# Output projection of one streaming-encoder layer: seven half products a row pair instead of eight, with token sums kept where the residual lay

## The chip, the cores and the metric

The kernel runs on one core of one Trainium2 chip. The metric is device time in microseconds for one call. Three runs of the kernel before took 1586.69, 1587.35 and 1587.35 us (median 1587.35). The profiled execution of the same kernel took 1586.78 us; from its first to its last instruction, its span, are 1585.1 us. Engines are named as in the profile: PE is the matrix engine (its weight loads are PEld), DVE the vector engine, ACT the scalar engine, POOL GpSimd, SP the queue that issues transfers.

## What is computed

One layer acts on 1056 tokens (1024 of a prompt, 32 of a sample) with 1024 channels. Only this part matters here:

```
merged = sigmoid(ga) * (ya @ w_br_att) + sigmoid(gm) * (ym @ w_br_mlstm)
x = x + gt1 * (merged @ w_out)            # the output projection
h2 = rmsnorm(x, g_ffn) * (1 + sc2) + sh2
g, up = split(h2 @ w_gate_up)             # the gated network follows
x = x + gt2 * ((silu(g) * up) @ w_down)
```

## The kernel before

Everything is kept transposed: 128 channels on the partitions, tokens along a row. The tokens are cut in three tiles of 352 (`TILES`, here t0, t1, t2; t2 holds 320 prompt and 32 sample tokens), the 1024 channels in eight blocks j of 128. A product in full precision is made from reduced ones: every weight and every operand is split into a high part (a rounding copy on ACT, L380) and a low part (what is left, a subtraction on DVE, L381). For each k block PE then does three passes: high weight by high operand, low weight by high operand, high weight by low operand (`PASSES`). A *unit* (L418) is one row block j times one token tile: 8 k blocks by 3 passes, 24 matmuls of 352 columns. A *half product* is four k blocks, 12 matmuls.

Weights come through a planner, `Weights`. A block has a load (SP, into one of 3 `wraw` buffers), a split (ACT and DVE, into `wsp` tiles of four k blocks, 4 of them) and a number of uses. When PE's program reaches a block (`W.use`), the planner emits the split of blocks up to `W.ahead` further on, as far as 4 `wsp` tiles hold them. `W.ahead` is 2 in the output projection and 4 after it. ACT, DVE and POOL each run their instructions strictly in the order in which the program emits them; only PE's order and theirs is written by hand, by emission.

Side work (`Side`) is a generator that is stepped while PE's matmuls are emitted: `side.start(gen, steps, ticks, delay)` spreads its steps over so many ticks, and there is a tick for every two k blocks, 6 matmuls. `side.drain` emits what is left at once.

The stages around the change, in order:

- *Merge* (L1626 on). For each j, a gate pair comes back from memory, and so does the residual `x2[j]`, all 1056 tokens (L1633). Two half units a tile, three DVE operations (L1639, L1641, L1642), then the result is split into `merged[j]` (L380, L381).
- *Output projection* (L1835 on). First all eight rows on t0, then all eight rows on t1 and t2: 24 units. After each unit DVE adds the product, times the gate `gt1`, onto the residual (L1842; this is called a *take* below; on t2 it is two pieces, 320 and 32 tokens), ACT squares the row (L1845, L1848), POOL adds the square to a sum (L1850), and SP stores the row to `xres` (L1861).
- *Second norm* (`second_norm`, L1672). For a tile: PE sums the squares over channels (`statistics`, L1662, and for the last row's square L1664), POOL takes the root, PE and ACT spread it over the partitions (L230, L233), and for each j DVE multiplies (L1694), ACT scales, shifts (L1697) and rounds (L1699), and DVE makes the low part (L1719) of `h2[j]`. For t0 it runs beside the projection's units on t1 and t2 (15 steps over 50 ticks); for t1 and t2 behind them, followed by `early_forms`, the operand sums of the gated network.

`xq` are four tiles that hold the residual of rows p and p+4 side by side. `h2` are eight `slots` buffers, taken when the second norm first needs them.

Of the kernel before, what the change touches and what calls it, by code (L numbers as in the profile page):

```python
# [17 lines left out]
P = 128  # L18
# [121 lines left out]
def hybrid_stream_step(  # L140
# [1428 lines left out]

    for w in w_merge + w_o[0] + w_o[1] + [w for ws in w_f for w in ws]:  # L1570
        W.add(w)
# [76 lines left out]
    sq_last = {}  # L1648
    h2 = []

# [21 lines left out]
    def second_norm(tiles):  # L1672
# [8 lines left out]
        for i, (lo, hi) in enumerate(tiles):  # L1681
# [41 lines left out]
    a_d = dr.tile([NF, P, T], F32, name="a_d")  # L1723
    thirds = [slice(lo, hi) for lo, hi in TILES]


# [107 lines left out]

    for pi, tiles in enumerate(parts):  # L1835
        if pi == 1:
            job = side.start(second_norm(parts[0]), 15, 50)
        for j in range(KD):
            for lo, hi in tiles:
                pt = unit(w_o[pi][j], 0, merged, lo, hi)  # L1840
                for c, a, b in col_segments(lo, hi):
                    dve.scalar_tensor_tensor(x2[j][:, a:b], pt[:, a - lo:b - lo], gt1[:, c, j:j + 1], x2[j][:, a:b],  # L1842
                                             op0=ALU.mult, op1=ALU.add)
                if j == 0:
                    act.activation(ss[:, lo:hi], x2[j][:, lo:hi], AF.Square)  # L1845
                else:
                    sq = third_tile()
                    act.activation(sq, x2[j][:, lo:hi], AF.Square)  # L1848
                    if j < KD - 1 or pi == 0:
                        pool.tensor_tensor(ss[:, lo:hi], ss[:, lo:hi], sq, op=ALU.add)  # L1850
                        if j == KD - 1:
                            sq_last[lo] = None
                    else:
                        sq_last[lo] = sq
                        if (lo, hi) == TILES[1]:


                            side.drain(job)
                            job = side.start(chain(second_norm(parts[1]), early_forms()), 9, 10)
            a, b = tiles[0][0], tiles[-1][1]  # L1860
            sp.dma_start(xres[j][:, a:b], x2[j][:, a:b])  # L1861

# [507 lines left out]
```

## Time and profile before

| what | value |
|---|---|
| median of three runs | 1587.35 us |
| the profiled execution | 1586.78 us |
| its span | 1585.1 us |
| PE busy | 1564.8 us, 10181 matmuls |
| DVE, ACT, POOL busy | 1107.0, 787.6, 420.5 us |
| granted PE clock over the span | 0.999 |
| output projection, first to last take | 797.7 to 889.1 us |

Busy times and shares are those of the profile's page; the line numbers there are those of the kernel before. A row of the timeline gives the start (us from the span's start), the length, the engine, the line, the operation, what it writes and reads, how many instructions are merged in it, and the engine's idle time before it with what ended that. Matmuls overlap: one of 352 columns lasts about 0.32 us, but the next starts half as much later.

### The profile page before, as it was taken

What the parts mean: (1) busy time and instruction counts of PE and PEld (TensorE: products, weight loads), DVE (VectorE), ACT (ScalarE), POOL (GpSimd) and SP (SyncE); (2) the same over time, 40 slices, a digit from 0 to 9 for tenths busy, and PEclk for the clock granted to TensorE, in tenths of its full rate; (3) what the DMA queues carried; (4) which work ended last, traced back from release to release, by engine and by line L of the source; (5) the groups of instructions that cost most, each with busy time, mean ns of one, the idle gap of its engine ahead of it and who ended that gap; (6) DMA issues with size and microseconds to landing.
All of it is one profiled execution on the core that took longest, in us unless ns stands there. A gap on an engine that the chain in (4) does not pass through costs nothing.

```text
span 1585.1 us, 27255 instructions
## 1 busy us (share of the span) xinstructions
PE 1564.8 (99%) x10181; PEld 1548.1 (98%) x10181; DVE 1107.0 (70%) x2270; ACT 787.6 (50%) x1730; POOL 420.5 (27%) x439
## 2 busy tenths in 40 slices
PE   8999999999999999999999999999999999999997
PEld 8999999999999999999999999999999999999997
DVE  3865655556767845446655699888898986799755
ACT  4765554544555545444434646544445444545443
POOL 0433343442223411000012100665665750000000
PEclk9999999999999999999999999999999999999999
DMA  9322233243122323575353312222232227427444
GB/s 376 131 76 78 88 104 98 93 132 106 42 91 74 88 78 102 120 275 173 112 157 113 94 55 67 82 77 98 68 93 83 69 89 248 137 80 253 129 137 156
DMA packets 176481, 187.08 MB, mean 118 GB/s; under 512 B 11766, under 2 KB 141466, under 8 KB 176222
## 3 DMA queue, kind: packets, MB, share of 16 engines
q1 hardware_dynamic: 173686, 183.50, 36.7%
q10 hardware_dynamic: 2664, 1.85, 0.4%
q8 instruction: 80, 1.31, 0.4%
q14 instruction: 51, 0.42, 0.1%
HBM read 151.15 MB, written 34.17 MB: 117 GB/s over the span
## 4 chain that ended last, share of the span: by engine, by line
PE 92%; DVE 4%; ACT 3%; issue 1%; POOL 0%; DMA 0%; ACTq 0%; DVEq 0%; POOLq 0%
PE mm L418 41%; PE psb L1903 18%; PE mm L1903 11%; PE psb L2285 3%; PE mm L971 3%; PE mm L2285 2%; PE psV L876 2%; PE psb L2149 2%; PE mm L329 2%; PE psS L817 1%; PE psT L844 1%; PE mm L2149 1%; DVE st L831 1%; PE psV L1205 1%; PE psT L1207 1%
## 5 line engine op out<-in xcount | busy, mean ns | idle before, releaser
L418 PE MATMUL mm<-s,wsp 128*128 128x352 f32 x4104 | 686.9, 324 | 0.3 <-DVE s L688 0.3
L418 PEld LDWEIGHTS mm<-s,wsp 128*128 128x128 f32 x4104 | 657.2, 188 | 2.1 <-DVE s L688 0.5
L381 DVE TENSOR_TENSOR wsp<-wraw,wsp 128x512 fp32r<-128x512 f32 (+1 forms) x280 | 236.1, 860 | 112.4 <-ACT wsp L380 110.4
L1903 PE MATMUL psb<-s,wsp 128*128 128x352 f32 x1611 | 271.4, 322 | 0.7 <-ACT wsp L380 0.7
L380 ACT ACTIVATE wsp<-wraw 128x512 fp32r<-128x512 f32 x336 | 199.7, 617 | 143.6 <-PE psb L1903 45.4
L1903 PEld LDWEIGHTS psb<-s,wsp 128*128 128x128 f32 x1611 | 260.6, 188 | 1.0 <-ACT wsp L380 1.0
L1903 PE MATMUL mm<-s,wsp 128*128 128x352 f32 x933 | 159.2, 322 | 0.7 <-DVE row L1941 0.7
L1903 PEld LDWEIGHTS mm<-s,wsp 128*128 128x128 f32 x933 | 151.2, 188 | 1.1 <-ACT wsp L380 1.0
L837 POOL TENSOR_SCALAR st<-st,mx 128x640 f32<-128x640 f32 (+5 forms) x72 | 53.3, 741 | 182.9 <-DVE mx L836 164.9
L1298 DVE CUSTOM_DVE_ANT_0 junk<-wa,t 128x512 bf16<-128x512 f32 x128 | 95.4, 746 | 2.8 <-DMA wa<-in_w_mod_dram 1.7
L381 POOL TENSOR_TENSOR wsp<-wraw,wsp 128x512 fp32r<-128x512 f32 x56 | 74.5, 1350 | 51.5 <-ACT wsp L380 49.2
L831 DVE CUSTOM_DVE_ANT_0 st<-psS,bias 128x640 f32<-128x640 f32 (+5 forms) x72 | 44.5, 618 | 57.9 <-PE psS L817 41.2
L832 ACT ACTIVATE st<-st,mx 128x640 f32<-128x640 f32 (+5 forms) x72 | 47.9, 666 | 63.7 <-DVE mx L831 63.6
L1850 POOL TENSOR_TENSOR t<-t,sl 128x352 f32<-128x352 f32 x19 | 18.0, 949 | 213.1 <-ACT sl L1848 213.1
L851 ACT ACTIVATE pT<-psT 128x640 fp32r<-128x640 f32 (+3 forms) x80 | 38.6, 493 | 64.2 <-PE psT L844 49.7
L2258 POOL TENSOR_TENSOR fst<-fst,mhalf 128x6 f32<-128x6 f32 x1 | 2.3, 2314 | 221.1 <-DVE fst L2257 221.1
L856 DVE TENSOR_TENSOR pT<-psT,pT 128x640 fp32r<-128x640 f32 (+3 forms) x80 | 44.0, 558 | 22.1 <-ACT pT L851 22.1
L1511 POOL TENSOR_TENSOR wraw<-wraw,raw 128x512 f32<-128x512 f32 x33 | 55.8, 1703 | 0.9
L971 PE MATMUL mm<-s,s 128*128 128x264 f32 (+3 forms) x432 | 54.5, 283 | 0.0
L2285 PE MATMUL psb<-s,wsp 128*128 128x352 f32 x330 | 54.2, 324 | 0.0
L2285 PEld LDWEIGHTS psb<-s,wsp 128*128 128x128 f32 x330 | 53.1, 188 | 0.1
L971 PEld LDWEIGHTS mm<-s,s 128*128 128x128 f32 (+1 forms) x432 | 51.9, 179 | 0.5
(381 smaller groups left out, 2457.5 us busy)
## 6 DMA issues: line engine op xcount, KB each, us to landing
wraw<-in_w_in_dram SPq DMA_DIRECT2D x37, 512.0 KB, 3.7
wraw<-in_w_gate_up_dram SPq DMA_DIRECT2D x33, 512.0 KB, 3.9
wa<-in_w_mod_dram SPq DMA_DIRECT2D x64, 256.0 KB, 2.7
wraw<-in_w_down_dram SPq DMA_DIRECT2D x32, 512.0 KB, 4.2
a_d<-t SPq DMA_DIRECT2D x22, 528.0 KB, 2.8
g_d<-t SPq DMA_DIRECT2D x16, 528.0 KB, 3.5
t<-g_d SPq DMA_DIRECT2D x16, 528.0 KB, 4.6
s<-in_w_ada_dram SPq DMA_DIRECT2D x16, 512.0 KB, 7.9
```

The source lines that it names most:

```text
L380: act.activation(dst[:, 0], src, AF.Copy)
L381: eng.tensor_tensor(dst[:, 1], src, f(dst[:, 0]), op=ALU.subtract)
L418: pe.matmul(pt[:, :hi - lo], wt[(w0 + k) // 4][:, a, (w0 + k) % 4], xt[k][:, b, lo:hi], start=(k == 0 and q == 0), stop=(k == n - 1 and q ...
L831: dve.tensor_tensor_reduce(so, sv, bi, -1.0, 3.0e38, ALU.add, ALU.min, mx[:n, 1:2])
L832: act.activation(st[:n, :w], st[:n, :w], AF.Exp, bias=mx[:n, 1:2], scale=-1.0, accum_out=mx[:n, 2:3])
L837: pool.tensor_scalar(st[:n, :w], st[:n, :w], mx[:n, 3:4], 1.0, op0=ALU.mult, op1=ALU.mult)
L971: pe.matmul(pt[:n, :wd], hs[k][:, a, i * P:i * P + n], whl[b][:, k, :wd], start=(k == 0 and q == 0), stop=(k == KD - 1 and q == 2))
L1298: dve.tensor_tensor_reduce(junk, wa, crow[:, c], 1.0, 0.0, ALU.mult, ALU.add, at)
L1511: self.eng.tensor_tensor(a(dst), a(x), a(y), op=op)
L1903: pe.matmul(acc, wt[:, a, k], x[k][:, b], start=(start and not onto and k == 0 and q == 0), stop=(stop and k == 3 and q == 2), skip_group_ ...
L2149: pe.matmul(acc, wt[k // 4][:, u, k % 4], piece_of[k, i][:, v], start=(k == 0 and q == 0), stop=(k == KP - 1 and q == 2))
L2285: pe.matmul(acc, wt[(k - k0) // 4][:, u, (k - k0) % 4], piece_of[k, 2][:, v], start=(k == 0 and q == 0), stop=(k == NF - 1 and q == 2))
```

## The change

Six of the eight rows, in the pairs (0, 4), (1, 5), (2, 6), are done two rows at a time. On t1 and t2 the pair's work is a two-by-two block product: two rows by two token tiles, over two halves of the channels, eight half products. The changed kernel does it with seven, by sums of weight blocks (`s1` to `s4`, made by `OutSeven.form`) and sums of token tiles (`T1` to `T4`, made by `sum_forms`), with results added onto each other in PSUM (`onto=True`). On t0 the pair still takes four half products. Rows 3 and 7 (`ALONE`) keep whole units.

The tokens' sums need merged values of t1 and t2 in full precision. The merge therefore writes them into `x2[j]`, where the residual used to be, and makes the sums in place during its last three rows (p = 0, 1, 2; p = 3 follows). They are then split into the `h2` buffers, which are taken right after the merge, by a side job `token_forms` of 19 steps over 22 ticks. Only t0 of the residual is loaded ahead; t1 and t2 are reloaded from memory when a piece's sums have been split (`form_low`, at T4). A take now happens for every half result that a row needs: nine for a pair where there were six. The planner's blocks for the pairs are half-blocks of one `wsp` tile, with one or two uses, and `W.ahead` is still 2 there. The second norm of t0 starts in the third pair, 15 steps over 14 ticks after a delay of 2.

```diff
+            def block(src, names=(), ld=lambda: None, uses=1):
+                def split(_):
+                    for n in names:
+                        form(n)
+                    t = wsplit_tile()
+                    split_to(t, src())
+                    return [t]
+                return [ld, split, uses, None, 1]
+
+            self.blocks = [
+                block(lambda: a(0, 0), ld=lambda: load(0), uses=2),
+                block(lambda: a(0, 1), ld=lambda: load(1), uses=2),
+                block(lambda: self.s["s2"], ("s1", "s2")),
+                block(lambda: a(1, 0)),
+                block(lambda: self.s["s3"], ("s3",)),
+                block(lambda: self.s["s1"], ("s4",)),
+                block(lambda: a(1, 1), uses=2),
+                block(lambda: self.s["s4"]),
+            ]
...
-        sp.dma_start(x2[j], x_t[j])
+        sp.dma_start(x2[j][:, :NT], x_t[j][:, :NT])
...
-            dve.tensor_tensor(ga[:, lo:hi], ga[:, lo:hi], gm[:, lo:hi], op=ALU.add)
-            split_to(mg[:, :, lo:hi], ga[:, lo:hi])
+            o = ga if lo == 0 else x2[j]
+            dve.tensor_tensor(o[:, lo:hi], ga[:, lo:hi], gm[:, lo:hi], op=ALU.add)
+            split_to(mg[:, :, lo:hi], o[:, lo:hi])
+            if j > 4:
+                sum_forms(j - 5, (("T1", "T3"), ("T2",), ("T4",))[TILES.index((lo, hi))])
...
+    def form_low(n, p, src, dst):
+        dve.tensor_tensor(dst[:, 1], src, f(dst[:, 0]), op=ALU.subtract)
+        if n == "T4":
+            for j in (p, p + 4):
+                sp.dma_start(x2[j][:, NT:], x_t[j][:, NT:])
...
+    def out_pair(j, u):
+
+        a00, a01, s2, a10, s3, s1, a11, s4 = seven_o[j].blocks
...
+        c = mmt()[:, :NT]
+        half(a00, ops["00"], c, stop=False)
+        half(a00, ops["B11"], u)
+        take(j, t2, u, False)
+        half(a01, ops["10"], c, start=False)
+        take(j, t0, c)
+        store(j, *t0)
+        take(j, t2, half(a01, ops["B21"], mmt()[:, :NT]))
...
+        half(s2, forms_o["T2"], u, onto=True)
+        take(j, t1, u, False)
+        c = mmt()[:, :NT]
+        half(a10, ops["00"], c, stop=False)
+        half(s3, forms_o["T3"], u, onto=True)
+        take(j + 4, t1, u, False)
...
+        v = half(s1, forms_o["T1"], mmt()[:, :NT])
+        take(j + 4, t1, v)
+        half(a11, ops["10"], c, start=False)
+        take(j + 4, t0, c)
+        store(j + 4, *t0)
+        if j == 2:
+            jobs.append(side.start(second_norm(parts[0]), 15, 14, 2))
+        half(a11, forms_o["T4"], u, onto=True)
+        take(j + 4, t2, u)
+        store(j + 4, NT, T)
+        half(s4, ops["B22"], v, onto=True)
+        take(j, t1, v)
+        store(j, NT, T)
+
+    job = side.start(token_forms(), 19, 22)
+    for w, j in zip(w_o[0], ALONE):
+        take(j, TILES[0], unit(w, 0, merged, *TILES[0]))
+        store(j, *TILES[0])
+    for j in range(3):
+        out_pair(j, (ps_s() if j % 2 == 0 else ps_t())[:, :NT])
+    for w, j in zip(w_o[1], ALONE):
+        for t in parts[1]:
+            take(j, t, unit(w, 0, merged, *t))
+            if j == ALONE[-1] and t == TILES[1]:
+                side.drain(jobs[0])
+                job = side.start(chain(second_norm(parts[1]), early_forms()), 9, 10)
+        store(j, NT, T)
```

How the order of instructions moves, at three places. First DVE, where the merge ends and the projection begins. Before (`L381 wsp` is the low part of a weight block, `L1842` a take, `L381 s` the low part of a merged row):

```order
L1642 TENSOR_TENSOR t_1171_8644<-t_1171_8644,t_1172_8645 128x352
L381 TENSOR_TENSOR s_1173_8649<-t_1171_8644,s_1173_8649 128x352
L381 TENSOR_TENSOR wsp_1185_8760<-wraw_1152_8432,wsp_1185_8760 128x512
L381 TENSOR_TENSOR wsp_1186_8761<-wraw_1152_8432,wsp_1186_8761 128x512
L1842 SCALAR_TENSOR_TENSOR x2_1083_7842<-mm_1188_8768,amod2_177,x2_1083_7842 128x352
L381 TENSOR_TENSOR wsp_1189_8796<-wraw_1164_8545,wsp_1189_8796 128x512
L381 TENSOR_TENSOR wsp_1190_8797<-wraw_1164_8545,wsp_1190_8797 128x512
L1842 SCALAR_TENSOR_TENSOR x2_1084_7843<-mm_1192_8804,amod2_177,x2_1084_7843 128x352
```

And now (`L1686` makes a token sum, `L1897` is the take, `L1945` the low part of a token sum, `wsp_1196` the first half-block of the first pair):

```order
L381 TENSOR_TENSOR s_1173_8657<-x2_1086_7845,s_1173_8657 128x352
L1686 TENSOR_TENSOR x2_1085_7844<-x2_1085_7844 128x352
L381 TENSOR_TENSOR wsp_1193_8780<-wraw_1152_8432,wsp_1193_8780 128x512
L381 TENSOR_TENSOR wsp_1194_8781<-wraw_1152_8432,wsp_1194_8781 128x512
L1686 TENSOR_TENSOR x2_1086_7845<-x2_1086_7845 128x352 x4
L1897 SCALAR_TENSOR_TENSOR x2_1086_7845<-mm_1195_8786,amod2_177,x2_1086_7845 128x352
L381 TENSOR_TENSOR wsp_1196_8819<-wraw_1164_8549,wsp_1196_8819 128x512
L1945 TENSOR_TENSOR s_1185_8771<-x2_1083_7842,s_1185_8771 128x352 x2
L1945 TENSOR_TENSOR s_1189_8775<-x2_1083_7842,s_1189_8775 128x352
L1897 SCALAR_TENSOR_TENSOR x2_1086_7845<-mm_1197_8822,amod2_177,x2_1086_7845 128x352
L381 TENSOR_TENSOR wsp_1201_8860<-wraw_1164_8549,wsp_1201_8860 128x512
```

Five token sums now stand ahead of the first take, and the low parts of the pair's weights stand one by one between takes and the low parts of token sums. Second, ACT where the second pair begins in the changed kernel (`L1906` squares a row after a take, `L380` is the high part of a weight half-block; `wsp_1218` and `wsp_1222` are a00 and a01, `wsp_1225` is s2, `wsp_1229` is a10):

```order
L1906 ACTIVATE sl_1216_9050<-x2_1083_7842 128x352
L1906 ACTIVATE sl_1217_9068<-x2_1083_7842 128x352
L380 ACTIVATE wsp_1218_9072<-wraw_1211_8992 128x512
L1906 ACTIVATE sl_1219_9088<-x2_1083_7842 128x352
L380 ACTIVATE wsp_1222_9094<-wraw_1211_8992 128x512
L380 ACTIVATE wsp_1225_9127<-t_1223_9123 128x512
L1906 ACTIVATE sl_1226_9143<-x2_1084_7843 128x352
L1906 ACTIVATE sl_1228_9162<-x2_1084_7843 128x352
L380 ACTIVATE wsp_1229_9165<-wraw_1214_9018 128x512
```

Before, a square and two high parts of a whole block alternate there, and the block is needed a unit later; now a half-block's high part stands behind the squares of takes that PE's previous half product but one releases. Third, DVE in the last unit pair, row 7, with the second norm of t0 (`L1754` its multiplication, `L1779` its low part) around the take of row 7 on t1 (`mm_1282`):

```order
L381 TENSOR_TENSOR wsp_1279_9602<-wraw_1262_9447,wsp_1279_9602 128x512
L381 TENSOR_TENSOR wsp_1280_9603<-wraw_1262_9447,wsp_1280_9603 128x512
L1754 TENSOR_TENSOR x2_1086_7845<-x2_1086_7845,t_1184_8770 128x352
L1779 TENSOR_TENSOR s_1187_8773<-x2_1085_7844,s_1187_8773 128x352
L1754 TENSOR_TENSOR x2_1083_7842<-x2_1083_7842,t_1184_8770 128x352
L1779 TENSOR_TENSOR s_1188_8774<-x2_1086_7845,s_1188_8774 128x352
L1754 TENSOR_TENSOR x2_1084_7843<-x2_1084_7843,t_1184_8770 128x352
L1779 TENSOR_TENSOR s_1189_8775<-x2_1083_7842,s_1189_8775 128x352
L1754 TENSOR_TENSOR x2_1085_7844<-x2_1085_7844,t_1184_8770 128x352
L1779 TENSOR_TENSOR s_1190_8776<-x2_1084_7843,s_1190_8776 128x352
L1897 SCALAR_TENSOR_TENSOR x2_1086_7845<-mm_1282_9610,amod2_177,x2_1086_7845 128x352
```

In the kernel before, that norm was spread over all of the second part, and about one of its operations stood between two takes; now eight of them stand in a row ahead of this one.

More of the change, by code (lines that the diff above doesn't have):

```diff
@@ L1568, in hybrid_stream_step @@
     w_d1 = [[weight([down(a, b, j)], b - a, 1) for a, b in chunks] for j in range(KD)]
-    for w in w_merge + w_o[0] + w_o[1] + [w for ws in w_f for w in ws]:
+    for w in w_merge + w_o[0] + [w for x in seven_o for w in x.blocks] + w_o[1] + [w for ws in w_f for w in ws]:
         W.add(w)
@@ L1628, in hybrid_stream_step, with sum_forms @@
     merged = []
+    thirds = [slice(lo, hi) for lo, hi in TILES]
+    def sum_forms(p, names):
+        x, y = x2[p], x2[p + 4]
+        one, two = thirds[2], thirds[1]
+        forms = {"T1": (x[:, one], x[:, two], x[:, one]), "T3": (x[:, two], y[:, two], x[:, two]),
+                 "T2": (y[:, two], y[:, two], x[:, one]), "T4": (y[:, one], y[:, one], y[:, two])}
+        for n in names:
+            o, u, v = forms[n]
+            dve.tensor_tensor(o, u, v, op=ALU.subtract)
     for j in range(KD):
@@ L1648, in hybrid_stream_step @@
     sq_last = {}
-    h2 = []
+    h2 = [slot([P, 2, T], F32R) for _ in range(KD)]
     def third_tile():
@@ L1723, in hybrid_stream_step @@
     a_d = dr.tile([NF, P, T], F32, name="a_d")
-    thirds = [slice(lo, hi) for lo, hi in TILES]
     FORMS = [[None] * 4 for _ in range(15)]
@@ L1833, in hybrid_stream_step @@
     normed = {}
[L1835 to L1861, printed above, removed]
@@ new lines, in take @@
+    def take(j, t, pt, last=True):
+        lo, hi = t
+        for c, a, b in col_segments(lo, hi):
+            dve.scalar_tensor_tensor(x2[j][:, a:b], pt[:, a - lo:b - lo], gt1[:, c, j:j + 1], x2[j][:, a:b],
+                                     op0=ALU.mult, op1=ALU.add)
+        if not last:
+            return
+        rows_done[lo] = rows_done.get(lo, 0) + 1
+        if rows_done[lo] == 1:
+            act.activation(ss[:, lo:hi], x2[j][:, lo:hi], AF.Square)
+        else:
+            sq = third_tile()
+            act.activation(sq, x2[j][:, lo:hi], AF.Square)
+            if rows_done[lo] < KD or lo == 0:
+                pool.tensor_tensor(ss[:, lo:hi], ss[:, lo:hi], sq, op=ALU.add)
+                sq = None
+            if rows_done[lo] == KD:
+                sq_last[lo] = sq
@@ new lines, in store, with token_forms @@
+    def store(j, a, b):
+        sp.dma_start(xres[j][:, a:b], x2[j][:, a:b])
+    rows_done, jobs = {}, []
+    forms_o = {}
+    def token_forms():
+        one, two = thirds[2], thirds[1]
+        where = {"T1": (0, one), "T3": (0, two), "T2": (4, two), "T4": (4, one)}
+        home = {"T2": (0, two), "T3": (0, one), "T1": (4, one), "T4": (4, two)}
+        sum_forms(3, ("T1", "T3"))
+        yield
+        sum_forms(3, ("T2", "T4"))
+        yield
+        order = [(n, 0) for n in ("T2", "T3", "T1", "T4")]
+        order += [(n, p) for n in ("T2", "T3", "T1", "T4") for p in range(1, 4)]
+        behind = []
+        for n, p in order:
+            dp, c = where[n]
+            hp, hc = home[n]
+            src, dst = x2[p + dp][:, c], h2[p + hp][:, :, hc]
+            forms_o.setdefault(n, [None] * 4)[p] = dst
+            act.activation(dst[:, 0], src, AF.Copy)
+            if behind:
+                behind.pop()()
+            behind.append(lambda n=n, p=p, src=src, dst=dst: form_low(n, p, src, dst))
+            yield
+        behind.pop()()
@@ new lines, in form_low, with half @@
+    def form_low(n, p, src, dst):
[3 more added lines that the diff above has]
+                sp.dma_start(x2[j][:, NT:], x_t[j][:, NT:])
+    def half(w, x, acc, start=True, stop=True, onto=False):
+        wt, = W.use(w)
+        for k in range(4):
+            for q, (a, b) in enumerate(PASSES):
+                pe.matmul(acc, wt[:, a, k], x[k][:, b], start=(start and not onto and k == 0 and q == 0),
+                          stop=(stop and k == 3 and q == 2), skip_group_check=onto)
+            if k % 2 == 1:
+                side.tick()
+        W.used(w)
+        return acc
```

34 lines of the change are left out of this document (31 added, 3 removed).

## The prediction

> **What bounds the kernel now.** I read the page first, then the busy times of the output projection by stretches, then its groups of instructions, then the timeline where the merge ends.
>
> ```profile
> PE 1564.8 (99%) x10181; PEld 1548.1 (98%) x10181; DVE 1107.0 (70%) x2270; ACT 787.6 (50%) x1730; POOL 420.5 (27%) x439
> ...
> PE 92%; DVE 4%; ACT 3%; issue 1%; POOL 0%; DMA 0%; ACTq 0%; DVEq 0%; POOLq 0%
> ```
>
> PE is the bound: 99% busy, 92% of the chain that ended last. In the projection, the stretches (columns: PE, PEld, DVE, ACT, POOL busy; granted clock; DMA share; GB/s) show no gap in PE and the others half idle:
>
> ```profile
> 797.00:830.00 33.00, 33.00 (x208) 33.00 (x207) 18.77 (x27) 12.82 (x25) 6.66 (x7) 1.00 0.60 178
> 830.00:860.00 30.00, 30.00 (x191) 29.98 (x190) 12.46 (x25) 10.27 (x20) 6.69 (x7) 1.00 0.34 112
> 860.00:890.00 30.00, 30.00 (x193) 30.00 (x192) 16.08 (x35) 13.71 (x27) 6.70 (x7) 1.00 0.34 107
> ```
>
> So each matmul removed is worth its pace, and each wait that PE gets is lost whole. The question is only whether the new order feeds PE in time.
>
> **What is removed.** The groups of 760 to 960 us give the pace:
>
> ```profile
> L418 PE MATMUL mm<-s,wsp 128*128 128x352 f32 x1075 | 174.5, 323 | 0.0
> ```
>
> 174.5 us / 1075 = 0.162 us a matmul. Three pairs save one half product of 12 each: 36 x 0.162 = **5.8 us**. A half product is 1.95 us, a unit 3.9.
>
> **What is added, and its price.** The timeline around the first take gives the links of the chain by which a weight block reaches PE:
>
> ```profile
> 795.63 0.53 DVE L381 TENSOR_TENSOR s<-t,s 128x352 fp32r<-128x352 f32 x1 [0.56 <-ACT s L380]
> 796.15 1.29 DVE L381 TENSOR_TENSOR wsp<-wraw,wsp 128x512 fp32r<-128x512 f32 x2
> ...
> 797.75 0.58 DVE L1842 SCALAR_TENSOR_TENSOR x<-mm,amod,x 128x352 f32<-128x352 f32 x1 [0.30 <-PE mm L418]
> 798.43 0.50 ACT L1845 ACTIVATE t<-x 128x352 f32<-128x352 f32 x1 [1.79 <-DVE x L1842]
> 798.83 1.14 ACT L380 ACTIVATE wsp<-wraw 128x512 fp32r<-128x512 f32 x2
> 799.48 1.29 DVE L381 TENSOR_TENSOR wsp<-wraw,wsp 128x512 fp32r<-128x512 f32 x2 [1.15 <-ACT wsp L380]
> ...
> 801.59 0.58 DVE L1842 SCALAR_TENSOR_TENSOR x<-mm,amod,x 128x352 f32<-128x352 f32 x1 [0.81 <-PE mm L418]
> 802.78 0.95 POOL L1850 TENSOR_TENSOR t<-t,sl 128x352 f32<-128x352 f32 x1 [158.24 <-ACT sl L1848]
> 803.26 1.62 DVE L381 TENSOR_TENSOR wsp<-wraw,wsp 128x512 fp32r<-128x512 f32 x2 [1.08 <-ACT wsp L380]
> ```
>
> From it: DVE to ACT 0.10; ACT's square holds it 0.40; a high part lasts 0.62 (two in 1.14, so 0.52 apart); ACT to DVE 0.03; a low part lasts 0.69 and holds DVE 0.60; a take 0.58, holding DVE 0.5. Beside POOL's addition the two low parts take 1.62 in place of 1.29. More holds, from later rows:
>
> ```profile
> 832.97 0.71 DVE L1842 SCALAR_TENSOR_TENSOR x<-mm,amod,x 128x320 f32<-128x320 f32 x2 [0.85 <-PE mm L418]
> 917.05 1.08 DVE L1739 TENSOR_TENSOR sl<-sl,x 128x352 f32<-128x352 f32 x2
> ...
> 918.48 0.52 DVE L1739 TENSOR_TENSOR sl<-x 128x352 f32<-128x352 f32 x1
> 918.91 0.52 DVE L1752 TENSOR_TENSOR s<-sl,s 128x352 fp32r<-128x352 f32 x1
> L1433 DVE TENSOR_TENSOR t<-wraw,wraw x8: 684/686/693, 1372.8 to 1466.0; 128x512 f32<-128x512 f32 x8
> ```
>
> A two-piece take 0.71; a 352-column sum or low part holds DVE 0.43, one that needs the one before it 0.56; a weight sum, by the down projection that sums weight blocks in the same way, lasts 0.69.
>
> The changed order has 32 more 352-column and 12 more 512-column two-input operations on DVE, 9 more takes (three of them in two pieces) and 16 more rounding copies on ACT: about 32 x 0.43 + 12 x 0.6 + 6 x 0.5 + 3 x 0.71 = 26 us of DVE in a stretch where it is busy 47 of 93 us. As a total that hides. It does not hide by order: a pair's block is a half-block, PE spends 1.95 us on one with a single use, the planner is at most one block ahead, and its split stands in line behind takes that wait for PE. Once PE waits for a high part, it also waits for the low part: its second pass needs it, so 0.03 + 0.69 - 0.16 = **0.56** more, or 0.95 when POOL adds beside it.
>
> *First pair*, on the clock of before. Unit boundaries on PE are near 797.55 and 801.39 (takes at 797.75 and 801.59, each 0.04 after the end of a pass of 0.32 whose successor starts 0.16 after it); a weight load is wanted 0.16 earlier, so a00 at 801.23. DVE now has one sum before the low parts that stood at 796.15 and four behind (0.43 + 3 x 0.56): first take at 799.85, square at 800.5, high part of a00 done 801.55: 0.3 late, plus 0.56. Then s2: three low parts (1.3), take, square, high and low part of a01 (805.8), four low parts (1.75), the two-piece take (0.7), two sums (1.4), high part done 810.3. PE has used a00 and a01 twice each and wants s2 at 801.55 + 0.56 + 4 x 1.92 = 809.8: 0.5 late, plus 0.56. Then a10: its high part stands on ACT behind the square of the next two-piece take, which DVE reaches after s2's low part, two low parts, a take and another: done 814.65 against 812.8, 1.9 late, plus 0.56. Then s3: 0.95, plus 0.56; s1: 0.2. Together **6.1** (4.5 to 7.5, by one step of 0.5 to 0.7 more or less in the queue).
>
> The reload stands in this too: the two-piece take, at 807.5, needs x2[0] back. Its transfer can go when T1's low part is done, near 803.6. Nearest rows:
>
> ```profile
> t<-g_d SPq DMA_DIRECT2D x13, 528.0 KB, 4.4
> ...
> x<-in_x_dram SPq DMA_DIRECT2D x3, 528.0 KB, 7.2
> ```
>
> The reload has 352 KB, two thirds of these: 3 to 5 us, landing 806.6 to 808.6. I take it as just in time; at the far end it adds 1.1, inside the 7.5.
>
> *Second and third pair.* No token sums are left, DVE has room, but two places in each run the same chain against one half product: a00 behind the square of the take of T4, and a10 behind that of B21. From the end of the pass: 0.04 + 0.71 (take) + 0.10 + 0.40 (square) + 0.62 + 0.03 = 1.90. The pass ends 0.32 after its start, the load is wanted 1.92 after it: 0.3 late, plus 0.56 or 0.95 (POOL adds the same square just then). s3's low part behind its sum: 0.57. Per pair 0.3 + 0.3 + 0.57 + 2 x (0.56 to 0.95) = 2.3 to 3.1; **5.6** for two. Row 3's whole block, behind the last pair in the same way: **0.8** (0.6 to 1.0).
>
> *Second norm of t0.* Its 15 steps now go into 14 ticks of 6 matmuls, 0.97 us a step, in place of 50. Rows on what a step needs:
>
> ```profile
> 853.15 0.50 ACT L1699 ACTIVATE s<-x 128x352 fp32r<-128x352 f32 x1
> 853.56 0.48 ACT L1848 ACTIVATE sl<-x 128x352 f32<-128x352 f32 x1
> 853.95 0.67 ACT L1697 ACTIVATE x<-x,amod 128x352 f32<-128x352 f32 x1
> 854.64 0.50 ACT L1699 ACTIVATE s<-x 128x352 fp32r<-128x352 f32 x1
> ```
>
> 0.69 and 0.41, 1.1 us of ACT a row, more than a step; and weight splits and squares stand between. What is late next is the statistics of t1: PE's L1664 matmul needs the square of row 7. From the broadcast's transposes to that matmul PE has 60 matmuls, 9.7 us. ACT has a square and the copy (1.1), the wait for DVE's first product (1.0), seven rows (7.7), a square and two high parts (1.4), the wait while DVE makes their low parts before the next product (1.8), the square itself (0.5): 13.5. PE waits **3.5** (2.0, if the two waits cover each other, to 4.2). Behind it in PE's queue stands the rest of row 7 on t2, then the gated network.
>
> At no cost: the merge loads a third of the residual, the stores are cut differently, eight residual loads of 528 KB become eight of 176 and eight of 352, at a DMA share of 0.60 or less. If that cover went, a w_out block would land late: the second of pair 1 is issued behind the last reloads, some 10 us before its first sum, against the 4 to 7 us of the rows above.
>
> *Sum:* -5.8 + 6.1 + 5.6 + 0.8 + 3.5 = +10.2. On the profiled execution (1586.8: 1585.1 of span and 1.7 around it) that is 1597.0, on the median of 1587.35 it is 1597.5. Forecast **1597**. With all low ends +5.9, with all high ends +13.1: 1593 to 1601 for this case.
>
> **A rule that speaks against the change.** The clock column reads 1.00 all through the projection, but here are the rows of PE's first work and of the end:
>
> ```profile
> 5.00:10.00 5.00, 4.87 (x23) 1.00 1.03 414
> 10.00:15.00 5.00, 5.00 (x44) 1.00 1.03 407
> 1580.00:1586.00 6.00, 0.00 (x0) 0.55 0.56 188
> ```
>
> After an idle start, PE makes 23 matmuls in its first 5 us and 44 in the next; at the end, idle again, the grant is 0.55. So an idle stretch of some microseconds seems to cost about (44 - 23) / 44 x 5 = 2.4 us of pace afterwards. The Trainium skill, in "TensorE: Matmul & The Clock Gate" (Why this matters for your kernels), says that a PE gap of more than about 3 us halves the clock again; by that the wait of the statistics, if over its bound, would cost those us more, and by these rows it may. No row shows a gap of 2 to 4 us in mid-kernel.
>
> **Rivals.** *The full gain* (other side): the split chain is not on PE's path, since DVE's and ACT's shares leave room and PE's gaps are absorbed: 1587.35 - 5.8 = 1581.6. Faster from the point where the waits sum under 5.8, a third of mine. For: no PE gap in 93 us before, where the same blocks alternate. Against: there a block was a unit ahead (the low parts of 799.48 serve a unit that starts at 801.39). *Half the waits*: the chains of 1.90 + 0.32 against 1.92 are so close that 0.3 less in each removes the first lateness, and s2's row keeps a margin; then 3.5 + 2.5 + 0.4 + 2 = 8.4, less 5.8: about 1590. *A colder PE or a late reload*: 10.2 plus 2.4 and up to 3 more for the reloads: 1600 to 1603. That fewer matmuls are not issued is excluded: the order has 8220 of 352 columns against 8256.
>
> **How the numbers follow.** Forecast 0.56, full gain 0.09, half the waits 0.15, colder or late 0.20. This kernel's measurement can tell 0.2%, 3.2 us, from no change: 1584.2 to 1590.5. The full gain gives faster 0.09; half the waits splits, 0.08 within; the rest is slower, 0.83. Range 1589 to 1603: it leaves out the full gain and the ends of the others.
>
> **What would show it.** PE's waits in the profile of the changed kernel: psS and mm of the half products waiting for ACT and DVE `wsp`, some 20 times, 0.2 to 2 us each, summing to 12, with half of it in the first pair; and one wait of psV for ACT's square of 2 to 4 us. Fewer than 6 us of PE waits between 793 and 900, or a take that waits for the reload, would make me wrong in size; the granted clock under 1.00 there would decide for the colder PE.

## The result: 1601.12 us, 0.9% slower

| | before | after |
|---|---|---|
| median, runs | 1587.35 us, 6 runs (1586.69 to 1587.52) | 1601.12 us, 6 runs (1600.40 to 1601.83) |
| the profiled execution | 1586.78 us | 1600.70 us |
| its span | 1585.1 us | 1599.0 us |

The ratio is 1.0088, with a 95% interval from 1.0075 to 1.0101. The forecast was 1597, slower, with a range from 1589 to 1603.

In the profile after, PE's waits in the output projection, in groups (engine, line, what it waited for: us in total, times, longest):

```profile
PE mm L1956 <- DVE wsp L381: 3.8, 6, 1.0
PE psV L1726 <- ACT sl L1906: 3.7, 1, 3.7
PE mm L1956 <- ACT wsp L380: 1.4, 1, 1.4
PE psS L1956 <- ACT wsp L380: 1.1, 2, 0.7
PE psS L1956 <- DVE wsp L381: 0.9, 3, 0.3
PE psT L1956 <- DVE wsp L381: 0.3, 1, 0.3
PE mm L418 <- DVE wsp L381: 0.3, 1, 0.3
```

Before, the same view of this stretch was empty. There are fourteen short waits for halves of weight blocks, where some twenty with a sum of 12 us were forecast, and the one long wait of the statistics. The short ones sum to 7.8 here, but their sizes are too small: ends of matmuls are modelled, so a pause counts only from the modelled end of the pass before, and some are not shown at all. The timeline of PE tells it by the starts:

```profile
796.83 4.80 PE L418 MATMUL mm<-s,wsp 128*128 128x352 f32 x29
801.65 0.43 PE L1956 MATMUL mm<-s,wsp 128*128 128x352 f32 x1
802.38 2.03 PE L1956 MATMUL mm<-s,wsp 128*128 128x352 f32 x11 [0.30 <-DVE wsp L381]
804.24 2.08 PE L1956 MATMUL psS<-s,wsp 128*128 128x352 f32 x12
...
814.91 0.43 PE L1956 MATMUL mm<-s,wsp 128*128 128x352 f32 x1 [1.42 <-ACT wsp L380]
815.64 2.04 PE L1956 MATMUL mm<-s,wsp 128*128 128x352 f32 x11 [0.30 <-DVE wsp L381]
...
826.89 2.44 PE L1956 MATMUL mm<-s,wsp 128*128 128x352 f32 x13
829.95 2.03 PE L1956 MATMUL mm<-s,wsp 128*128 128x352 f32 x11 [0.62 <-DVE wsp L381]
...
839.66 0.43 PE L1956 MATMUL mm<-s,wsp 128*128 128x352 f32 x1
841.05 2.03 PE L1956 MATMUL mm<-s,wsp 128*128 128x352 f32 x11 [0.96 <-DVE wsp L381]
...
875.85 2.11 PE L1956 MATMUL mm<-s,wsp 128*128 128x352 f32 x12
...
878.33 0.41 PE L418 MATMUL mm<-s,wsp 128*128 128x352 f32 x1
879.03 4.96 PE L418 MATMUL mm<-s,wsp 128*128 128x352 f32 x29 [0.29 <-DVE wsp L381]
...
893.82 0.28 PE L1724 MATMUL psV<-ones,t 128*128 128x1 f32 x2
897.75 0.58 PE L1726 MATMUL psV<-ones,sl 128*128 128x1 f32 x2 [3.65 <-ACT sl L1906]
...
909.61 0.28 PE L1724 MATMUL psV<-ones,t 128*128 128x1 f32 x2
...
973.68 1.60 PE L2056 MATMUL psb<-s,wsp 128*128 128x352 f32 x9
```

The row of 814.91 holds one pass; the next starts 0.73 later, where 0.16 is normal. So this pause for a low part is 0.57, of which 0.30 is shown. The same places before (the statistics of t1, those of t2, and the first product of the gated network's second part):

```profile
886.23 0.28 PE L1662 MATMUL psV<-ones,t 128*128 128x1 f32 x2
...
895.48 0.28 PE L1662 MATMUL psV<-ones,t 128*128 128x1 f32 x2
...
959.55 1.76 PE L1903 MATMUL psb<-s,wsp 128*128 128x352 f32 x10
```

The account follows from these starts, at 0.16 a matmul and 1.92 a half product.

- *First pair.* It is due at 796.83 + 29 x 0.16 = 801.47 and ends at 826.89 + 1.92 = 828.81. That is 27.34 for 11 half products (21.12): 6.2 of waits.
- *Second and third pair.* They end at 875.85 + 1.92 = 877.77, 48.96 later, for 42.24: 6.7.
- *Up to the statistics of t1.* These begin 7.6 later than before. The saved matmuls are 5.8, so all waits up to there are 13.4. Beside the 6.2 and 6.7 above, some 0.6 belong to row 3 (its first passes start at 878.33 and 879.03, 0.70 apart, and the one behind them 0.1 late) and 0.1 to a later start; that is 13.6, the same within the rounding of these steps.
- *From the statistics of t1 to those of t2.* 15.79 in place of 9.25, so 6.54 more. The gap is 3.65 of it. The other 2.9 go somewhere else, and the stretches behind the gap in the profile after say where (PE, PEld, DVE, ACT, POOL busy; clock; DMA share; GB/s):

```profile
897.70:903.70 6.00, 5.95 (x24) 5.95 (x25) 1.76 (x8) 2.13 (x5) 1.01 (x1) 0.50 0.05 21
903.70:910.00 6.30, 6.30 (x44) 6.28 (x42) 4.65 (x8) 5.60 (x10) 0.00 (x0) 1.00 0.66 185
```

The granted clock is 0.50 behind the gap: 24 matmuls in 6 us (ten of them the statistics' one-column ones), then 44 in 6.3. The trace's clock record has it at 0.5 for 6.83 us, from 896.86 on. PE idles in the first 0.9 of them; half of the other 5.9 is 3.0, against the 2.9 that are missing.

- *Behind that.* From the statistics of t2 to the gated network's second part both kernels take 64.07. The kernel after is 14.1 behind there and 13.9 at the end, so no more than 0.2 is won or lost anywhere else.

### The profile page after: what moved, and what is told of

Its sections match the earlier page's. It is cut to its first block, busy times and chain, and to the rows that moved or that the text cites. A ratio compares the mean times of both kernels' runs of the same rounds, so it can differ in the third digit from the quotient of the medians.

```text
span 1599.0 us, 27237 instructions
## 1 busy us (share of the span) xinstructions
PE 1567.1 (98%) x10145; PEld 1544.8 (97%) x10145; DVE 1131.2 (71%) x2326; ACT 794.9 (50%) x1746; POOL 420.4 (26%) x439
## 4 chain that ended last, share of the span: by engine, by line
PE 86%; DVE 6%; ACT 4%; DMA 2%; issue 1%; POOL 0%; SPq 0%; ACTq 0%; DVEq 0%; POOLq 0%
PE mm L418 35%; PE psb L2056 18%; PE mm L2056 11%; PE psb L2438 3%; PE mm L971 3%; PE mm L2438 2%; PE psV L876 2%; PE psb L2302 2%; PE psS L817 1%; DVE wsp L381 1%; PE psT L844 1%; DMA s<-in_w_ada_dram 1%; PE mm L2302 1%; PE mm L1956 1%; ACT wsp L380 1%
## 5 line engine op out<-in xcount | busy, mean ns | idle before, releaser
L418 PE MATMUL mm<-s,wsp 128*128 128x352 f32 x3672 | 619.6, 325 | 0.6 <-DVE wsp L381 0.3
L418 PEld LDWEIGHTS mm<-s,wsp 128*128 128x128 f32 x3672 | 589.7, 189 | 2.6 <-DVE s L688 0.5
L381 DVE TENSOR_TENSOR wsp<-wraw,wsp 128x512 fp32r<-128x512 f32 (+1 forms) x268 | 226.8, 861 | 114.5 <-ACT wsp L380 112.0
L380 ACT ACTIVATE wsp<-wraw 128x512 fp32r<-128x512 f32 x324 | 193.4, 617 | 144.3 <-PE psb L2056 44.1
L2056 PEld LDWEIGHTS psb<-s,wsp 128*128 128x128 f32 x1611 | 260.6, 188 | 1.0 <-ACT wsp L380 1.0
L2056 PE MATMUL mm<-s,wsp 128*128 128x352 f32 x933 | 159.2, 322 | 0.7 <-DVE row L2094 0.7
L2056 PEld LDWEIGHTS mm<-s,wsp 128*128 128x128 f32 x933 | 151.2, 188 | 1.1 <-ACT wsp L380 1.0
L381 POOL TENSOR_TENSOR wsp<-wraw,wsp 128x512 fp32r<-128x512 f32 x56 | 74.0, 1340 | 51.9 <-ACT wsp L380 49.6
L380 ACT ACTIVATE s<-x 128x352 fp32r<-128x352 f32 x84 | 37.4, 487 | 35.0 <-DVE x L1702 35.0
L380 ACT ACTIVATE wsp<-t 128x512 fp32r<-128x512 f32 x44 | 27.4, 630 | 52.7 <-DVE t L1570 19.8
```

The source lines that it names most:

```text
L380: act.activation(dst[:, 0], src, AF.Copy)
L381: eng.tensor_tensor(dst[:, 1], src, f(dst[:, 0]), op=ALU.subtract)
L418: pe.matmul(pt[:, :hi - lo], wt[(w0 + k) // 4][:, a, (w0 + k) % 4], xt[k][:, b, lo:hi], start=(k == 0 and q == 0), stop=(k == n - 1 and q ...
L2056: pe.matmul(acc, wt[:, a, k], x[k][:, b], start=(start and not onto and k == 0 and q == 0), stop=(stop and k == 3 and q == 2), skip_group_ ...
```

## Experiments

Each was timed in turn with the kernel before on the same chip, whose median was 1587.0 to 1587.2 there. An experiment is compared with the change's 1601.12, whose own kernel before took 1587.35. The change's six times lie in two groups 1.1 apart, and its median between them (the last section says why), so differences of medians are good to about 1 us; where more is needed, the profiles are compared.

| run | what | median, us | ratio to before, 95% interval |
|---|---|---|---|
| e1 | 18 unused matmuls in the gap | 1598.19 | 1.0072 (1.0058 to 1.0086) |
| e2 | 6 unused matmuls in the gap | 1599.49 | 1.0081 (1.0067 to 1.0094) |
| e3 | planner two blocks ahead | 1593.77 | 1.0041 (1.0028 to 1.0053) |
| e4 | no token sums, no reload | 1595.68 | 1.0055 (1.0042 to 1.0068) |
| e5 | a gap put into the kernel before | 1595.63 | 1.0052 (1.0038 to 1.0066) |
| e6 | squares behind high parts | 1596.29 | 1.0056 (1.0043 to 1.0068) |
| e7 | e3, and 16 unused matmuls | 1591.93 | 1.0030 (1.0019 to 1.0042) |
| e8 | two pairs, cover at both ends | 1585.86 | 0.9992 (0.9983 to 1.0001) |
| e9 | e8 with three orders changed | 1585.36 | 0.9988 (0.9979 to 0.9997) |

### Is it the gap that slows PE's clock?

e1 fills most of the gap with matmuls that nobody reads; e2, with 6 in place of 18, fills less of it.

```diff
         sq = sq_last[lo]
+        if lo == NT:
+            idle = mmt()
+            for i in range(18):
+                pe.matmul(idle[:, :NT], merged[0][:, 0, :P], merged[1][:, 0, :NT], start=(i == 0), stop=(i == 17))
         for i, (a, b) in enumerate(subs):
```

> The changed kernel with 18 extra matmuls of 352 columns into an unused bank, issued just ahead of the statistics of t1, at the place where PE waited 3.65 us for ACT's square of row 7. Nothing else is touched; their result is not used. 18 x 0.162 = 2.9 us lie inside the wait. My theory (the 3.65 us gap itself brings the granted clock to 0.5 for the 6.8 us that follow, which costs about half of them less what was idle anyway, some 3 us): with the gap cut to about 0.7 us the granted clock stays at 1.00 between 895 and 905, and 18 matmuls MORE make the kernel 2.5 to 3.5 us FASTER than the change: about 1598. Rival (the slow matmuls after the gap are fed late, or the clock falls for another reason at that place): the time stays at 1601 +- 0.7, and the clock row stays under 1.00.

> As the run with 18 extra matmuls, with 6 of them: 1.0 us of the 3.65 us is filled, and about 2.7 us of idle PE is left. It asks from what length of gap the clock falls. If the fall needs a gap near the 3.65 us seen here, the clock stays at 1.00 and the time is about 1598, as with 18; if a gap of 2.7 us suffices, the clock row shows 0.5 for some us again and the time stays at 1601 +- 0.7. If the loss grows with the gap, it lies between. The rival without a clock effect gives 1601 for this run and for the one with 18 alike.

With 18 more matmuls the kernel was 2.9 us faster than the change by the medians, 1598.19, as the theory had it. The rival, 1601, falls. But the clock row did not stay at 1.00. PE in e1, and the stretches around it:

```profile
893.75 3.06 PE L1726 MATMUL mm<-s,s 128*128 128x352 f32 x18
896.65 0.28 PE L1728 MATMUL psV<-ones,t 128*128 128x1 f32 x2
897.70 0.38 PE L1730 MATMUL psV<-ones,sl 128*128 128x1 f32 x2 [0.78 <-ACT sl L1910]
...
898.73 3.56 PE L418 MATMUL mm<-s,wsp 128*128 128x352 f32 x13
```

```profile
896.10:899.50 3.40, 2.62 (x22) 2.54 (x21) 2.43 (x7) 2.54 (x5) 0.00 (x0) 0.99 0.00 0
899.50:902.90 3.40, 3.40 (x13) 3.40 (x12) 1.64 (x6) 1.82 (x4) 1.01 (x1) 0.50 0.27 106
```

A gap of 0.78 and the statistics' one-column matmuls around it were still followed by 3.41 us at half clock, one stretch in place of two; that execution took 1599.66, 1.0 under the change's profiled 1600.70. The five times of e1 fall in two groups, 1598.1 to 1598.2 (three) and 1599.5 to 1599.7 (two); the profile is of the upper one. It fits that the lower group had no slow stretch, but no trace of such a run shows it. e2 lies between: its profile has a gap of 2.69 and one slow stretch, and its median 1599.49 is 1.6 under the change. So the loss is neither a matter of the gap alone nor of a sharp length; it comes in whole stretches. What one costs can be read from the statistics of t1 to those of t2, 9.25 before: e2 takes 13.66 with its gap of 2.69, e1 11.76 with its gap of 0.78, so in both 1.7 for a stretch in which PE has work throughout, half of its length.

e5 takes the gap to a place without the change.

```diff
+                    if j == KD - 1 and lo == NT:
+                        for _ in range(12):
+                            act.activation(sq, x2[j][:, lo:hi], AF.Copy)
                     act.activation(sq, x2[j][:, lo:hi], AF.Square)
```

> The kernel BEFORE, with 12 copies on ACT put ahead of its square of row 7 on t1 (they write the tile that the square writes next, so nothing else changes). In before, ACT is free some 1.5 us ahead of the statistics that read this square, so at 0.40 us a copy PE gets one gap of about 3.3 us (4.8 if a copy into the same tile takes 0.53), at a place without any other part of the change. This prices a gap by itself. My theory (a gap of this length is followed by two stretches of 3.41 us with the clock at 0.5): the time rises by the gap and 2.5 to 3 us more, so for 3.3 us to 1593, with the clock row under 1.00 behind the gap. Rival (the low clock came with the change, not with the gap): it rises by the gap alone, to about 1590.5, clock 1.00.

```profile
892.31 0.59 PE L1664 MATMUL psV<-ones,sl 128*128 128x1 f32 x2 [4.60 <-ACT sl L1851]
```

```profile
890.00:900.00 10.00, 7.69 (x30) 7.69 (x31) 2.68 (x7) 4.93 (x11) 1.01 (x1) 0.50 0.10 39
900.00:905.00 5.00, 5.00 (x35) 4.98 (x33) 2.91 (x6) 3.57 (x6) 0.00 (x0) 1.00 0.78 228
```

A copy into the same tile took longer than 0.40, so the gap was 4.6. The time rose by 8.5. In the profile, the way from the statistics of t1 to those of t2 is 17.50 in place of 9.25, so 3.65 more than the gap, and the clock is at 0.5 for 10.24 us, three stretches, in the first 2.6 of which PE idles. The rival, the gap alone, would be 1591.7. A gap costs its length and then PE's pace, whatever made it.

### Do the pairs wait because of an order, or of a rate?

e3 lets the planner split two blocks ahead of the one in use (`W.ahead` counts that one too, so 2 was one block ahead).

```diff
     job = side.start(token_forms(), 19, 22)
+    W.ahead = 3
```

> The changed kernel with the planner at most two blocks ahead in place of one in the output projection (W.ahead = 3 from its start; the four half-block buffers are the same). My theory (the waits of the pairs come from the order: a block's split stands behind a take that waits for PE, so it is a fraction of a us late again and again, while DVE and ACT have room in sum): nearly all waits of half products on wsp in pairs 2 and 3 go (5.6 us by my sum), in the first pair most of them are traded for one wait of about 3 us, since DVE now has the low parts of two blocks ahead of the token sums' low parts; the time falls by 6 to 9 us, to 1592 to 1595. The wait of 3.3 to 3.7 us on psV and the fall of the clock after it stay. Rival (a rate, not an order: half-blocks used once can't be split in 1.95 us beside takes and squares): the waits come back later in each pair, and the time falls by less than 3 us, to 1598 or more.

It took 7.4 us off, inside the forecast of 1592 to 1595, but not by the split expected. PE's two longest waits in e3:

```profile
PE psV L1726 <- ACT sl L1906: 3.5, 1, 3.5
PE psS L1956 <- DVE x L1897: 3.5, 2, 2.9
```

```profile
814.00:818.00 4.00, 1.13 (x8) 0.87 (x7) 3.22 (x6) 3.30 (x8) 0.21 (x1) 1.00 0.10 12
818.00:822.00 4.00, 4.00 (x17) 4.00 (x17) 3.75 (x9) 1.00 (x3) 0.00 (x0) 0.57 0.91 287
...
830.00:870.00 40.00, 40.00 (x251) 40.00 (x251) 27.55 (x48) 14.20 (x27) 9.92 (x10) 1.00 0.30 94
```

In pairs 2 and 3 PE is busy for 40.00 of 40 us: their 6.7 us were a matter of order and lead, nearly all of it (0.2 is left up to 871.44, where their last product ends). The first pair is no shorter (it ends at 828.99, in the change at 828.81). There DVE is busy for 3.22 of 4 us while PE waits 2.9 for a take of the bank that it adds onto, and the clock falls behind this gap too (17 matmuls in 4 us at 0.57). That take stands on DVE behind a low part that itself waited:

```profile
815.54 0.69 DVE L381 TENSOR_TENSOR wsp<-t,wsp 128x512 fp32r<-128x512 f32 x1 [0.78 <-ACT wsp L380]
...
817.02 0.58 DVE L1897 SCALAR_TENSOR_TENSOR x<-psS,amod,x 128x352 f32<-128x352 f32 x1
```

ACT began the high part that it waited for at 814.88, when PE's half product before the gap had ended; the profile gives that product as what released it. So an order (a take behind a split that waits for PE) is in this gap too, and not only DVE's load. Which of them weighs more isn't shown.

e6 changes one order on ACT alone.

```diff
-            act.activation(sq, x2[j][:, lo:hi], AF.Square)
-            if rows_done[lo] < KD or lo == 0:
-                pool.tensor_tensor(ss[:, lo:hi], ss[:, lo:hi], sq, op=ALU.add)
...
+            def square():
+                act.activation(sq, x2[j][:, lo:hi], AF.Square)
+                if rows_done[lo] < KD or lo == 0:
+                    pool.tensor_tensor(ss[:, lo:hi], ss[:, lo:hi], sq, op=ALU.add)
+            last = rows_done[lo] == KD
...
+            if last or j in ALONE:
+                side.flush()
+                square()
+            else:
+                side.later.append(square)
...
     def half(w, x, acc, start=True, stop=True, onto=False):
         wt, = W.use(w)
+        side.flush()
```

> The changed kernel with one order changed on ACT: the square that follows a take of the pairs is put behind the next block's high part instead of ahead of it (POOL's addition, which needs the square, moves with it). My theory (a block's high part comes through take, 0.10, square 0.40, high part 0.62, and the sum of 1.90 + 0.32 is 0.3 us over the 1.92 us of one half product): in pairs 2 and 3 and row 3 the 0.3 us of lateness of high parts go, and of the low part's 0.56 to 0.95 us about 0.46 stays; pairs 2 and 3 lose 2.5 to 3 us of waits, row 3 0.4, the first pair under 1: 1597 (1596 to 1598). Rival (ACT has room, the square is not on the way; takes and DVE alone make the blocks late): 1601 +- 0.7. The wait on psV stays 3.5 us or so, and the low clock behind it too.

1596.29, 4.8 us faster than the change and inside the theory's 1596 to 1598; the rival falls. PE in pair 2 of e6:

```profile
826.88 4.03 PE L1964 MATMUL mm<-s,wsp 128*128 128x352 f32 x24
...
839.09 2.03 PE L1964 MATMUL mm<-s,wsp 128*128 128x352 f32 x11 [0.33 <-DVE wsp L381]
```

Where the change pauses at 829.95, e6 runs 24 matmuls without a pause; the pause of 0.96 at a10 is 0.33. The first pair ends at 828.80, as in the change: the gain is in pairs 2 and 3 (3.6) and in row 3 (0.6), 4.2 of the 4.4 between the two profiled executions. So squares of 0.40 us ahead of high parts of 0.62 cost 4 us, since each stood between a take and a block that came some 0.3 us late because of it.

### What do the token sums cost?

e4 leaves the token sums, their splits and the reload out.

```diff
-        sp.dma_start(x2[j][:, :NT], x_t[j][:, :NT])
+        sp.dma_start(x2[j], x_t[j])
...
-            o = ga if lo == 0 else x2[j]
+            o = ga
...
-            if j > 4:
-                sum_forms(j - 5, (("T1", "T3"), ("T2",), ("T4",))[TILES.index((lo, hi))])
...
-    job = side.start(token_forms(), 19, 22)
+    for n, (h, t) in {"T1": (0, 1), "T2": (1, 1), "T3": (0, 2), "T4": (1, 2)}.items():
+        forms_o[n] = [merged[p + 4 * h][:, :, thirds[t]] for p in range(4)]
```

> The changed kernel without the token sums: the merge keeps its old output buffer and loads the whole residual, no T1 to T4 are made or split, nothing is reloaded, and the half products read pieces of the merged rows in their place (so this run leaves out part of the computation). The order of PE, the weight sums and the splits of weights stay. My theory: the first pair then behaves as the second does (about 2.8 us of waits in place of 6.1): 3.3 us faster than the change, 1597 to 1599. Rival A (the token sums and the reload are hidden, the waits come from the half-blocks alone): 1601 +- 0.7. Rival B (they cost more than the waits on PE near them, by the merge's last rows or by the reloads in the way of weight loads): 6 us or more faster, under 1595.5. The wait on psV and the low clock after it stay in all three.

5.4 us faster than the change by the medians and 4.5 by the profiled executions, more than the theory's 3.3 and short of rival B's 6; rival A falls. PE's first pair in e4:

```profile
799.73 2.40 PE L418 MATMUL mm<-s,wsp 128*128 128x352 f32 x14
801.97 2.08 PE L1954 MATMUL mm<-s,wsp 128*128 128x352 f32 x12
...
822.65 2.44 PE L1954 MATMUL mm<-s,wsp 128*128 128x352 f32 x13
```

No pause ahead of 801.97, and the pair ends at 824.57: 22.60 for 21.12, so 1.5 of waits in place of 6.2. (The pair also starts 0.5 later than in the change; the runs don't say why.) The token sums carry 4.7 of the first pair's 6.2, not the 3.3 of 6.1 that was expected. Their price lies on DVE, in whose queue the weights' low parts and the takes stand behind them, and no wait for the reload shows. In the change, the take that needs the reloaded row follows the token sums' low parts on DVE without a pause:

```profile
806.16 1.82 DVE L1945 TENSOR_TENSOR s<-x,s 128x352 fp32r<-128x352 f32 x4
807.90 0.69 DVE L1897 SCALAR_TENSOR_TENSOR x<-psS,amod,x 128x320 f32<-128x320 f32 x2
```

What the transfers would cost with less work on DVE was not tried.

### Are the two independent, and is there a version that wins?

e7 joins e3 and a fill of 16 matmuls.

> The changed kernel with both: the planner two blocks ahead in the projection (1593.8 by itself) and 16 unused matmuls of 352 columns ahead of the statistics of t1, 2.6 us of its 3.5 us gap. Theory of the clock: one or both of the two slow stretches of 3.41 us behind this gap go, 1.3 to 2.9 us: 1591 to 1592.5; the stretch behind the first pair's gap of 2.9 us stays. If the two effects were not independent, it stays at 1593.8 or rises.

1591.93, inside 1591 to 1592.5: 1.8 under e3. Its profile has one slow stretch of 3.41 us behind the statistics in place of two, and the one behind the first pair's gap, as expected. The gains stand side by side: 9.2 under the change, where e3 gained 7.4 and e1, with 18 matmuls, 2.9.

e8 takes what the others showed: splits ahead of the takes, four units on t0 ahead of the first pair for DVE's backlog, and eight units behind the pairs for ACT's second norm. T3, T1 and T4 are pulled by `need` as T2 is, and the job isn't drained at once.

```diff
-    ALONE = (3, 7)
+    ALONE = (2, 3, 6, 7)
...
-    seven_o = [OutSeven(j) for j in range(3)]
+    seven_o = [OutSeven(j) for j in range(2)]
...
-        half(s2, forms_o["T2"], u, onto=True)
+        half(s2, need("T2"), u, onto=True)
...
-        if j == 2:
-            jobs.append(side.start(second_norm(parts[0]), 15, 14, 2))
+        if j == 1:
+            jobs.append(side.start(second_norm(parts[0]), 15, 24, 2))
...
-    job = side.start(token_forms(), 19, 22)
+    job = side.start(token_forms(), 19, 37)
+    W.ahead = 3
...
-    for j in range(3):
+    for j in range(2):
```

> A version that gives the side work cover at both ends: two pairs by seven half products in place of three, rows 2, 3, 6 and 7 by whole blocks (four units on t0 ahead of the pairs, eight on t1 and t2 behind them), the planner two blocks ahead, each half product pulls the token sums that it needs and no more (19 steps in 37 ticks), the second norm of t0 in 24 ticks. It computes the whole result. 24 matmuls are saved, 3.9 us. Theory: no gap of over 2 us is left, the clock stays at 1.00 to the end; about 0.9 us of waits ahead of the first pair, 2 in it, 0.2 in the second, under 0.5 at the statistics, some 3 to 4 in all: 1586 to 1587.5, at or just under before. Rival (the half-blocks' waits go with the number of pairs, not with what lies ahead of and behind them): two thirds of 13.4 us remain, 9, less 3.9: 1592.

1585.86, just under the lower end of 1586: the rival's 1592 falls. The clock record has no slow stretch before PE's work ends. The ratio's interval just reaches 1, so against before this is not told from no change. e9 adds e6's order, the same for the whole rows, and a later start of the token sums. Against e8:

```diff
-    job = side.start(token_forms(), 19, 37)
+    job = side.start(token_forms(), 19, 31, 3)
...
-        take(j, TILES[0], unit(w, 0, merged, *TILES[0]))
+        pt = unit(w, 0, merged, *TILES[0])
+        W.advance()
+        take(j, TILES[0], pt)
```

> The two-pair version (1585.86 by itself) with three orders changed: squares of the pairs stand behind the next block's high part on ACT (worth 4.8 us in the changed kernel), the blocks of the four whole rows on t0 are split ahead of the take that they stood behind, and the token sums start three ticks later (19 steps in 31 ticks), so that their four dependent sums no longer stand ahead of the first take. It computes the whole result. Left of waits in the two-pair version: 0.3 ahead of the first pair as shown, 0.2 and 0.8 in it, 0.3 at the statistics, and low parts that are shown at half. Theory: 1.5 to 2 us of them go: 1584 +- 0.5, under before by 0.2%. Rival (what is left is DVE's rate in the first pair and moves to another place): 1585.5 to 1586, as the two-pair version.

1585.36: 1.9 under before and the fastest of all, but 0.5 under e8 where 1.5 to 2 were expected. That is the rival's outcome, or just under it. Its waits, and the stretch of the first pair:

```profile
PE psS L1964 <- ACT wsp L380: 1.6, 1, 1.6
PE psV L1726 <- ACT sl L1908: 0.3, 1, 0.3
```

```profile
797.00:830.00 33.00, 31.38 (x196) 31.13 (x196) 28.40 (x52) 16.86 (x36) 3.78 (x4) 1.00 0.51 160
```

The small waits went, and one of 1.6, for a high part, took their place in the first pair, where DVE is busy for 28.4 of 33 us. The kernel saves 24 matmuls, 3.9 us, and gains 1.9 (0.03% to 0.21% by the interval).

## Why the prediction was right in its direction and short in its size

| step | forecast | measured |
|---|---|---|
| 36 matmuls saved | -5.8 | -5.8 |
| first pair | 6.1 (4.5 to 7.5) | 6.2 |
| second and third pair | 5.6 (2.3 to 3.1 each) | 6.7 |
| row 3's block | 0.8 (0.6 to 1.0) | 0.6 |
| gap at the statistics of t1 | 3.5 (2.0 to 4.2) | 3.65 |
| slower clock behind the gap | not in the sum; 2.4 as a rival | 2.9 |
| sum | +10.2 | +14.2 by these steps, +13.9 by the profiled executions |

*The step that failed* is the sum's last: the clock. The forecast held a gap of 3.5 us, and the text beside it priced what such a gap does to the pace behind it, 2.4 us from the first rows of the kernel. But it kept this as a rival of 0.20, as if the two could part. The runs make them one case: whoever expects the gap has to expect the loss, and 10.2 + 2.4 gives 1599.4 on the profiled execution's time, which took 1600.7. By its own test, a clock row under 1.00, the colder PE decided; e1, e2 and e5 show that the gap is its cause. The Trainium skill's rule in "TensorE: Matmul & The Clock Gate" (Why this matters for your kernels) was borne out: the clock did fall behind a gap of 3.65 us. (It also fell behind shorter ones; see the last section.) With it in the sum the forecast would have been +12.6, against +13.9. The range reached to 1603 only because of this rival: the sum's own ends, 1593 to 1601, just miss 1601.12.

*The first pair* was right in size, and its parts were too: a00 0.85 late against 0.86, from the starts at 801.47 and 804.24, and by further starts 1.3 against 1.06 at s2, 2.3 against 2.46 at a10, 1.5 against 1.51 at s3. Its cause was weighed wrongly. The expectation of e4 took 2.8 of the 6.1 to be there without token sums; e4 shows 1.5, nearly all of it at the low parts of a10 and s3.

*The second and third pair* were short by 1.1. The mechanism held: chain of take, square, high part and low part against one half product, a wait for the low part behind each wait for a high part (0.57 against 0.56). e6 took the square out of it and 3.6 of the 6.7 went. The term that was too small is a low part beside POOL's additions. The wait for it was taken as 0.56 to 0.95, the last beside one addition. At a10, where two additions follow each other, the low part lasted 1.36 (DVE's row below) in place of 1.02, and the pass waited 1.2 (839.66 to 841.05, less 0.16):

```profile
838.62 1.84 POOL L1908 TENSOR_TENSOR t<-t,sl 128x352 f32<-128x352 f32 x2 [6.67 <-ACT sl L1906]
```

```profile
839.64 1.36 DVE L381 TENSOR_TENSOR wsp<-wraw,wsp 128x512 fp32r<-128x512 f32 x1 [1.08 <-ACT wsp L380]
```

*Row 3's block* was taken as the pairs' blocks and waited some 0.6, the low end.

*The statistics* waited 3.65 against 3.5. The prediction's own terms give more than the 3.5 that it took: 13.5 less 9.7 is 3.8. The reason was as given, the second norm's rows ahead of row 7, on both engines at once:

```profile
896.53 0.58 DVE L1897 SCALAR_TENSOR_TENSOR x<-mm,amod,x 128x352 f32<-128x352 f32 x1
...
897.20 0.50 ACT L1906 ACTIVATE sl<-x 128x352 f32<-128x352 f32 x1
```

PE had that product ready near 894.0. The take starts 2.5 later, behind the norm's operations on DVE, some of which wait for ACT; ACT ends the norm's row before the square when the take ends.

*The full gain* didn't come: the split chain was on PE's path, and even with the planner two blocks ahead (e3) 6.8 us of loss are left. *Half the waits*, about 1590, was reached neither by the change nor by e3 or e6. *The reload* was in time, as taken: the take at 807.90 starts without a pause.

## What to carry to other kernels

When a forecast contains a gap of the matrix engine of some microseconds, its sum must hold the pace lost behind it, here half of the time that PE works in the slow stretches, 1.7 us for a full one of 3.41 us; and unused matmuls that fill the gap can make a kernel faster, as in e1 and e7. Before a stage is given smaller blocks of work, look at how far ahead its planner is in time, not in blocks: half-blocks with one use halve the lead, and then a 0.4 us instruction in the wrong place of a queue, once a block, took 4 us of the 5.8 that the saved matmuls are worth. Work that fills an engine off the path needs matmuls of its own beside it, ahead and behind: two pairs with cover (e8, 1585.86) beat three without, the planner being two blocks ahead in both (e3, 1593.77). Which part of the cover did it was not taken apart.

## What the runs showed that I had not expected

The clock moves in steps of 3.41 us. All slow stretches in mid-kernel in the traces' clock records are 3.41, 6.83 or 10.24 us long, one, two or three steps, and from the first rise to any later change lie whole numbers of steps (887.47 us in the change, 260 of them). The change's six times fall in two groups, 1600.4 to 1600.7 and 1601.5 to 1601.8, and those of e1 and e7 do the same; the groups are 1.1 to 1.6 apart on the mean, where a full step at half clock costs 1.7. The mean granted clock that goes with each of the change's times fits one step more: 0.996 for all three of the lower group, 0.995 for all three of the upper, and one step is half of 3.41 in 1599, 0.001. The profiled execution is of the lower group, and no trace of an upper one shows the step. The Trainium skill, in "TensorE: Matmul & The Clock Gate" (Part 1: The HAM clock gate), names a free-running window of 3413 ns, and the traces agree with its length; it puts the fall after an idle window of about 3.4 us, and here less was enough: 2.9 us of gap in e3 brought one slow step, and in e1 0.78 us with the statistics' one-column matmuls around it. In both, less than 40% of the step before was spent on 352-column matmuls (in e1 0.6 us up to 896.65 and 0.7 from 898.73 on, of 3.41). Worked out from the starts in the same way, no full-clock step with 45% or more, in any trace's projection, was followed by a fall, each one with 36% or less was, and of two near 40% in e2 one was. Where between them it falls, the runs don't settle.
